# Channel shuffle on one core: eight buffers of 24 KB a partition become four of 48 KB, loaded whole and stored in halves, with the small tiles first

## The chip, the cores and the metric

One core of one Trainium2 chip runs the kernel. The time is the device time of one execution in microseconds (us), given as the median of the runs of one job; single runs of one kernel mostly agree within 0.3%. A profile records one such execution; its span is some 1.8 us shorter than the time. Ratios are the mean time of one kernel's fast runs over the mean of the other's fast runs in the same rounds on the same chip, with a 95% interval, so they are not quite the ratios of the medians that are quoted.

## The reference

The reference reorders channels: 65,536 rows (16 x 64 x 64) of 256 floats, in each of which 8 groups of 32 channels are interleaved.

```python
x = x.reshape(batch, h, w, groups, channels_per_group)   # 8 groups of 32
x = x.transpose(0, 1, 2, 4, 3)
x = x.reshape(batch, h, w, c)
```

No arithmetic is done. 67.11 MB are read and 67.11 MB written.

## The kernel before

Each tile takes 128 x q rows of x, q rows of 1 KB to a partition; in the text a "24 KB tile" is one with q = 24. SBUF and PSUM are two memories on the chip; a tile lies in SBUF, spread over 128 partitions. SP (the sync engine) issues the load. DVE (the vector engine) permutes 8 KB pieces from SBUF into PSUM, ACT (the scalar engine) copies them back in place, and ACT issues the store when all pieces of the tile are done. A DMA of a tile has 128 rows, one for each partition; a "row of 24 KB" below is such a row. In the packet records of the traces each row is one packet, and each DMA adds 16 packets of 4 bytes, here called completion writes, which tell its semaphore that the data have landed.

```python
_SIZES = [24] * 20 + [8, 24]
_BUFS = 8
_PIECE = 8
...
    for q in _SIZES:
        buf = pool.tile([P, biggest * c], F32, name="buf")
        nc.sync.dma_start(out=buf[:, : q * c], in_=rows(x_flat, first, q))
        for k in range(0, q, _PIECE):
            piece = buf[:, k * c : (k + _PIECE) * c]
            bounce = psum.tile([P, _PIECE * c], F32, name="bounce")
            nc.vector.tensor_copy(
                out=bounce.rearrange("p (i j g) -> p i j g", j=CPG, g=G),
                in_=piece.rearrange("p (i g j) -> p i j g", g=G, j=CPG),
            )
            nc.scalar.copy(out=piece, in_=bounce)
        nc.scalar.dma_start(out=rows(out_flat, first, q), in_=buf[:, : q * c])
```

A load into a buffer waits until the buffer's last store has landed. The 44 DMAs share eight completion semaphores (the landings in the trace), so a DMA may also have to wait for the one that had its semaphore last.

Of the kernel before, what the change touches and what calls it, by code (L numbers as in the profile page):

```python
# [1 line left out]

# [4 lines left out]


F32 = mybir.dt.float32
P = 128  # L10

_SIZES = [24] * 20 + [8, 24]
_BUFS = 8

_PIECE = 8


@with_exitstack
def kernel(
    ctx: ExitStack,  # L20
    tc: tile.TileContext,
    x: bass.AP,
    groups: bass.AP,
    out: bass.AP,
):
    nc = tc.nc
    b, h, w, c = x.shape
    G = int(groups)
    CPG = c // G
    assert G * CPG == c  # L30
    assert sum(_SIZES) * P == b * h * w
    biggest = max(_SIZES)

    x_flat = x.rearrange("b h w c -> (b h w c)")
    out_flat = out.rearrange("b h w c -> (b h w c)")

    pool = ctx.enter_context(tc.tile_pool(name="pool", bufs=_BUFS))
    psum = ctx.enter_context(
        tc.tile_pool(name="psum", bufs=2, space=bass.MemoryType.PSUM)
    )  # L40

    def rows(flat, first, q):

        return flat[first * c : (first + P * q) * c].rearrange("(p f) -> p f", p=P)

    ctx.enter_context(tc.manual_schedule(engines=None))
    first = 0
    for q in _SIZES:
        buf = pool.tile([P, biggest * c], F32, name="buf")
        nc.sync.dma_start(out=buf[:, : q * c], in_=rows(x_flat, first, q))  # L50
        for k in range(0, q, _PIECE):
            piece = buf[:, k * c : (k + _PIECE) * c]
            bounce = psum.tile([P, _PIECE * c], F32, name="bounce")
            nc.vector.tensor_copy(  # L54
                out=bounce.rearrange("p (i j g) -> p i j g", j=CPG, g=G),
                in_=piece.rearrange("p (i g j) -> p i j g", g=G, j=CPG),
            )
            nc.scalar.copy(out=piece, in_=bounce)  # L58
        nc.scalar.dma_start(out=rows(out_flat, first, q), in_=buf[:, : q * c])  # L59
        first += P * q  # L60


# [1 line left out]
_INS = ['x', 'groups']  # L64
_OUTS = [((16, 64, 64, 256), 'float32')]

_NUMBERS = {'groups': 8}


# [26 lines left out]
```

## Time and profile before

| | before |
|---|---|
| time, median of 3 | 317.66 us (317.65 to 317.87) |
| span of the profile | 315.9 us |
| DVE, ACT busy | 72%, 38% |
| both DMA queues, share of 16 engines | 99.3% |

The two queues are q1 (loads, issued by SP) and q10 (stores, issued by ACT). The list of waits of the compute engines (who waited for whom; us in total, times, longest; L58 is line 58 of the kernel) is worth a look, as it seems to say where time could be had:

```profile
ACT buf L58 <- DVE bounce L54: 115.3, 56, 5.6
ACT buf L58 <- DMA buf<-in_x_dram: 55.7, 4, 26.0
DVE bounce L54 <- ACT buf L58: 38.8, 4, 18.8
```

ACT once stood 26 us behind a load, and DVE then stood 18.8 us behind ACT.

### The profile page before, as it was taken

The page shows a single profiled execution, that of the slowest core. Times are in us where ns is not written, and L with a number is a line of the kernel's source. Part 1 is how long each engine was busy: PE and PEld are TensorE (multiplying, and loading weights), DVE is VectorE, ACT ScalarE, POOL GpSimd, SP SyncE. Part 2 cuts the span into 40 slices and gives each one's busy share as a digit, 9 for nine tenths or more (in the row PEclk, how much of TensorE's full clock was granted, in tenths as well). Part 3 has the DMA queues.
Part 4 walks back from the last instruction along what each step waited for, and adds up shares of the span by engine and source line. Part 5 has one row for each costly group of instructions (what it writes and reads, how often), then busy time and mean ns, then how long its engine had stood idle before and what let it go on. Part 6 is the DMA issues. An engine that isn't in the chain of part 4 may idle for free.

```text
span 315.9 us, 289 instructions
## 1 busy us (share of the span) xinstructions
DVE 227.9 (72%) x64; ACT 120.3 (38%) x65; POOL 0.2 (0%) x4
## 2 busy tenths in 40 slices
DVE  0699999959587685957008986999970299999900
ACT  0354455525252424330015416545500444555420
POOL 0000000000000000000000000000000000000000
DMA  8999999999999999999999999999999999999997
GB/s 296 439 442 380 436 429 433 433 439 433 423 442 433 426 442 426 426 442 426 433 436 427 433 436 436 433 426 437 433 423 448 423 429 444 429 423 433 439 432 302
DMA packets 6338, 134.24 MB, mean 425 GB/s; under 512 B 704, under 2 KB 704, under 8 KB 704
## 3 DMA queue, kind: packets, MB, share of 16 engines
q1 hardware_dynamic: 3168, 67.11, 49.9%
q10 hardware_dynamic: 3168, 67.11, 49.4%
q14 instruction: 2, 0.02, 0.0%
HBM read 67.11 MB, written 67.11 MB: 425 GB/s over the span
## 4 chain that ended last, share of the span: by engine, by line
DVE 54%; another core or an unknown queue 23%; issue 8%; ACT 5%; DMA 3%; DVEq 1%; ACTq 0%
DVE bounce L54 54%; ACT buf L58 5%; DMA buf<-in_x_dram 3%; DVEq L91 1%; ACTq L59 0%; DVEq L54 0%; ACTq L58 0%
## 5 line engine op out<-in xcount | busy, mean ns | idle before, releaser
L54 DVE COPY bounce<-buf 128x2048 f32<-128x2048 f32 x64 | 227.9, 3636 | 72.6 <-ACT buf L58 38.8
L58 ACT COPY buf<-bounce 128x2048 f32<-128x2048 f32 x64 | 119.0, 1866 | 171.1 <-DVE bounce L54 115.3
L58 ACT ACT_TABLE_LOAD x1 | 1.3, 1283 | 11.1 <-DMA buf<-in_x_dram 11.1
L77 POOL MEMSET const-bfloat16-1.0<- 128x1 bf16 x1 | 0.1, 102 | 0.0
L77 POOL MEMSET const-uint8-127<- 128x1 uint8 x1 | 0.1, 101 | 0.0
L77 POOL MEMSET const-float32-0.0<- 128x1 f32 x1 | 0.1, 99 | 0.2 <-issue 0.2
L77 POOL MEMSET const-float32-1.0<- 128x1 f32 x1 | 0.1, 98 | 0.0
## 6 DMA issues: line engine op xcount, KB each, us to landing
buf<-in_x_dram SPq DMA_DIRECT2D x21, 3072.0 KB, 58.4
out_dram<-buf ACTq DMA_DIRECT2D x21, 3072.0 KB, 24.2
buf<-in_x_dram SPq DMA_DIRECT2D x1, 1024.0 KB, 46.0
out_dram<-buf ACTq DMA_DIRECT2D x1, 1024.0 KB, 15.8
```

The source lines that it names most:

```text
L54: nc.vector.tensor_copy(out=bounce.rearrange("p (i j g) -> p i j g", j=CPG, g=G), in_=piece.rearrange("p (i g j) -> p i j g", g=G, j=CPG),)
L58: nc.scalar.copy(out=piece, in_=bounce)
L77: nc = _bacc.Bacc("TRN2", target_bir_lowering=False, num_devices=1)
L91: with _tile.TileContext(nc) as tc:
```

## The change

The intent is to issue fewer, longer loads, to let data flow out as soon as half a tile is ready, and to start computing earlier by taking the small tiles first. The bytes in SBUF stay 192 KB a partition.

```diff
-_SIZES = [24] * 20 + [8, 24]
-_BUFS = 8
+_SIZES = [8, 24] + [48] * 10
+_BUFS = 4
+
+_STORE = 24
 ...
-        for k in range(0, q, _PIECE):
-            ... permute a piece, copy it back
-        nc.scalar.dma_start(out=rows(out_flat, first, q), in_=buf[:, : q * c])
+        for a in range(0, q, _STORE):
+            b = min(a + _STORE, q)
+            for k in range(a, b, _PIECE):
+                ... permute a piece, copy it back
+            cols = slice(a * c, b * c)
+            nc.scalar.dma_start(
+                out=rows(out_flat, first, q)[:, cols], in_=buf[:, cols]
+            )
```

(The loop bodies are cut; they are the ones above. `b` of the shape is renamed to `n`.)

More of the change, by code (lines that the diff above doesn't have):

```diff
@@ L26 @@
     nc = tc.nc
-    b, h, w, c = x.shape
+    n, h, w, c = x.shape
     G = int(groups)
@@ L30 @@
     assert G * CPG == c
-    assert sum(_SIZES) * P == b * h * w
+    assert sum(_SIZES) * P == n * h * w
     biggest = max(_SIZES)
@@ L50 @@
         nc.sync.dma_start(out=buf[:, : q * c], in_=rows(x_flat, first, q))
-        for k in range(0, q, _PIECE):
-            piece = buf[:, k * c : (k + _PIECE) * c]
-            bounce = psum.tile([P, _PIECE * c], F32, name="bounce")
-            nc.vector.tensor_copy(
-                out=bounce.rearrange("p (i j g) -> p i j g", j=CPG, g=G),
-                in_=piece.rearrange("p (i g j) -> p i j g", g=G, j=CPG),
-            )
-            nc.scalar.copy(out=piece, in_=bounce)
-        nc.scalar.dma_start(out=rows(out_flat, first, q), in_=buf[:, : q * c])
+        for a in range(0, q, _STORE):
+            b = min(a + _STORE, q)
+            for k in range(a, b, _PIECE):
+                piece = buf[:, k * c : (k + _PIECE) * c]
+                bounce = psum.tile([P, _PIECE * c], F32, name="bounce")
+                nc.vector.tensor_copy(
+                    out=bounce.rearrange("p (i j g) -> p i j g", j=CPG, g=G),
+                    in_=piece.rearrange("p (i g j) -> p i j g", g=G, j=CPG),
+                )
+                nc.scalar.copy(out=piece, in_=bounce)
+            cols = slice(a * c, b * c)
+            nc.scalar.dma_start(
+                out=rows(out_flat, first, q)[:, cols], in_=buf[:, cols]
+            )
         first += P * q
```

## The prediction

> **What bounds the kernel now.** I read the page's strip of slices first, then the queues, then a table of stretches, the queues inside one short window, and last the waits of the load queue.
>
> ```profile
> span 315.9 us, 289 instructions
> DVE 227.9 (72%) x64; ACT 120.3 (38%) x65; POOL 0.2 (0%) x4
> ...
> DMA  8999999999999999999999999999999999999997
> ...
> q1 hardware_dynamic: 3168, 67.11, 49.9%
> q10 hardware_dynamic: 3168, 67.11, 49.4%
> ```
>
> DVE has 88 us to spare and ACT 195 us; the DMA row stands at 9 from the second slice to the last but one. Queue q1 (loads) and q10 (stores) together fill 49.9 + 49.4 = 99.3% of 16 engines over the span. The table of stretches (us, then busy time of DVE, ACT and POOL, clock, DMA share, GB/s) says where the rest is:
>
> ```profile
> 0.00:1.70 1.70, 0.00 (x0) 0.00 (x0) 0.20 (x4) 1.00 0.00 0
> 1.70:4.00 2.30, 0.00 (x0) 0.00 (x0) 0.00 (x0) 1.00 1.11 299
> 4.00:24.00 20.00, 12.95 (x4) 6.88 (x4) 0.00 (x0) 1.00 1.00 433
> 24.00:32.00 8.00, 8.00 (x3) 3.73 (x2) 0.00 (x0) 1.00 1.02 399
> 32.00:140.00 108.00, 85.89 (x25) 46.63 (x25) 0.00 (x0) 1.00 1.00 432
> 140.00:170.00 30.00, 10.48 (x3) 3.63 (x2) 0.00 (x0) 1.00 1.00 432
> ...
> 302.50:314.00 11.50, 0.00 (x0) 0.00 (x0) 0.00 (x0) 1.00 0.97 416
> 314.00:315.90 1.90, 0.00 (x0) 0.00 (x0) 0.00 (x0) 1.00 0.00 0
> ```
>
> The body runs at 432 GB/s whether loads run alone (4 to 24 us) or with stores. 134.2 MB at 432 GB/s is 310.7 us. Lost on top: 1.7 us before the first packet, 2.3 x (1 - 299/432) = 0.7 us of slow first packets, 8 x (1 - 399/432) = 0.6 us when stores set in, 0.4 us in the drain, 1.9 us after the last packet: 5.3 us, together 316.0 against a span of 315.9. Even between 140 and 170 us, where DVE works 10.48 of 30 us, DMA stays at 432. There ACT stands before a store: the built program has eight DMA completion semaphores, and a store that takes one over waits for the DMA that had it, here a load; the chain of waits has a hole of 25.46 us from 138.75. Loads fill that hole, so it costs nothing. The kernel is bound by DMA engines, and only those 5.3 us are not transfer.
>
> **How the two queues share an engine.** This decides the change, and the one 8 KB tile of the kernel before shows it. In a window in which that load runs against a store of 24 KB rows:
>
> ```profile
> q10 hardware_dynamic: 121, 2.58, 74.9%
> q1 hardware_dynamic: 113, 0.91, 26.8%
> ```
>
> Columns: packets, MB, share of 16 engines over 8 us (128 us of engine time). 2.58 MB are 105 rows of 24 KB, 0.91 MB are 111 rows of 8 KB: about one row of each in turn, while the bytes go 2.8 to 1. A row takes 0.749 x 128 / 105 = 0.913 us (24 KB) or 0.268 x 128 / 111 = 0.309 us (8 KB); the packet records read 912 and 309 ns. From the two: 603 ns for 16 KiB more is 37.7 ns a KiB, which leaves 309 - 8 x 37.7 = 7.5 ns a row. A 48 KB row should then take 48 x 37.7 + 7.5 ns = 1.82 us, if it goes as one packet.
>
> **What the Trainium skill says.** "DMA: Bandwidth & Descriptors", section "Queues, rings and completion order": each engine goes round-robin between queues at packet granularity. The trace agrees, and shows that a turn here is one row of the DMA (105 against 111), not the 9 to 17 descriptors that the page calls typical. Same page, "Where 436 GB/s comes from": a ceiling of 435.2 GB/s; the trace has 432 to 433, so there is under 1% to win in the body. Same page, "Why small descriptors are slow": a fixed cost for each packet; the trace has about 7.5 ns. "Perfetto Trace Analysis", section "DMA Optimizations": splitting DMAs may help "If DMA engines are generally idle"; here they are not, so splitting the store should not pay by itself.
>
> **The change part by part.**
> - Compute: the order of instructions shows the same 64 DVE copies (3.56 us from start to start) and 64 ACT copies (1.87 us). Nothing removed.
> - Bytes: the same. Loads: 21 of 24 KB rows and one of 8 KB become 10 of 48, one of 24, one of 8. Each engine has 8 of the 128 rows of a tile, so 160 rows of 24 KB become 80 of 48 KB: 80 x 7.5 ns = 0.6 us less. Ten fewer completion writes, 9 ns each in the packet records: 0.1 us less. Stores: 22 as before. Sum: **-0.7 us**.
> - Small tiles first: the first load (1 MB instead of 3) should land at about 11.0 - 8 rows x 0.603 = 6 us instead of 11, and the first store be issued at about 6 + 3.6 + 1.9 = 12 us instead of 23.7. It starts DVE 5 us earlier, beside a DMA queue that is full anyway: 0 us. The 1.7 and 1.9 us at the ends stay, the slow first packets too.
> - The end: a last tile of 48 KB instead of 24. It looks bad: DVE needs 6 x 3.56 = 21.3 us after its load. But a load is issued only when the tile four before it has been stored (in the program, load 12 waits for stores 13 and 14). Count from then, in time of one DMA engine: the six stores of tiles 9 to 11 are still to go, 6 x 7.3 = 43.8 us, and the last load, 8 x 1.82 = 14.6 us: 58.3 us of work that needs nothing from the last tile. Rows alternate, so the load is through after 8 x (1.82 + 0.91) = 21.8 us, and lands 3 us later at most (10.3 us for the first load of 7.3 us of rows). First half permuted at 24.8 + 10.7 + 1.9 = 37.4, second at 48.1. The engines come to them at 58.3 and 65.6. **Spare: some 20 and 17 us.** The end stays full.
> - The middle: the loads take two bytes for one of the stores, so a tile is loaded beside one of its two stores in 21.8 us, then 7.3 us of store alone: 29.1 us a tile, against 21.3 us of DVE. Loads get ahead until buffers stop them, as today; a queue always has work.
>
> Sum: 317.66 - 0.7 = **317.0 us**.
>
> **Rivals.**
> 1. *Loads and stores share bytes equally* (48 KB rows cut in pieces of 24 KB, or turns by bytes). Then loads lose their lead: the second store comes at about 26 us (second load landed at 13.5, three DVE copies, one ACT copy); until then loads, nearly alone, have moved about 70 KB a partition of 512 (21 us at 7.3 us for 24 KB). The other 442 at 14.6 us for 24 KB take 269 us, so the last load lands at some 291 to 295 us, as it never waits for a buffer. Then 21.3 + 1.9 us of permuting and 7.3 + 1.5 us for the last store: 323 to 327, most of it with idle engines. Time about **326**. Against it: the 8 KB rows above. For it: no row over 24 KB is in this trace.
> 2. *A new semaphore wait.* With 34 DMAs instead of 44 over eight semaphores the pairings change; a store held behind a load could leave both queues empty, since four buffers give loads fewer places. In the new program two stores take over a load's semaphore (store 14 after load 9, store 16 after load 10), both of loads issued four stores or more earlier. I expect waits of DVE and ACT, hidden as today; if one were bare, 5 to 10 us, 322 to 327.
> 3. *A faster start.* If an early store or shorter first load saved the lost start, at most the 1.3 us of slow packets: 315.7. Against it: the first packets wait whatever their length.
> 4. *DVE becomes the bound*: 228 us of 316; would need 80 us more. No.
>
> Load waits on stores exist already and are the throttle that keeps the order:
>
> ```profile
> SPq L50 <- DMA out_dram<-buf: 209.9, 14, 22.0
> ```
>
> 209.9 us of waiting in the load queue, with full engines: it costs nothing now, and should not after.
>
> **Range and chances.** The floor is 310 us of bytes plus about 5, so 2% less (311.3) is closed: 0.01. Rivals 1 and 2 together some 7%, and either makes it over 2% slower (324.0). The rest is within 2%. For the range: rival 3 and small row savings below (316.0), a us or two of gaps at buffer changes above (318.8).
>
> **What would show it.** Right: 1728 packets on q1 instead of 3168 (12 loads of 128 rows, and 16 completion writes each), two thirds of bytes to loads where both run, DMA at 432 to the last slices, the last load landing at about 265 us (73 us of engine work are left when it is issued, 58.3 and 14.6 for the last tile's stores, so that is at 314 - 73 = 241, and 24.8 more), the last store issued some 17 us before the engines come to it. Wrong: equal MB on q1 and q10 in every window, last load at 290 or later, zeros in the DMA row in the last three slices; or a hole in mid-run with ACT waiting before a store.

## The result, and the profile after

The changed kernel takes **317.78 us** (median of 4, 317.37 to 318.22), the kernel before 317.65 us in the same job. The ratio is 1.0003 (0.9986 to 1.0021): the same.

The changed kernel's page and its table of stretches (columns as in the prediction):

```profile
span 316.4 us, 251 instructions
DVE 228.0 (72%) x64; ACT 120.6 (38%) x65; POOL 0.2 (0%) x4
...
q1 hardware_dynamic: 1728, 67.11, 49.7%
q10 hardware_dynamic: 3168, 67.11, 49.3%
```

```profile
1.70:4.00 2.30, 0.00 (x0) 0.00 (x0) 0.00 (x0) 1.00 0.99 292
...
32.00:140.00 108.00, 99.83 (x29) 52.22 (x28) 0.00 (x0) 1.00 0.99 426
140.00:170.00 30.00, 22.21 (x7) 11.19 (x6) 0.00 (x0) 1.00 1.01 437
...
302.50:314.00 11.50, 0.00 (x0) 0.00 (x0) 0.00 (x0) 1.00 0.97 417
```

The number of load packets went from 3168 to 1728, so a row of 48 KB is one packet. The queues still fill 99.0% of the engines, start and drain have the rates of before (292 and 417 GB/s against 299 and 416), and the middle scatters from stretch to stretch (426, 437), but its mean from 4 to 302.5 us is 431 GB/s in both profiles. Within the bound, a lot did change. Over a stretch in which both queues always had work (52 to 92 us), the queues shared the engines like this (packets, MB, share):

```profile
q1 hardware_dynamic: 256, 11.80, 68.1%
q10 hardware_dynamic: 256, 5.51, 32.0%
```

Packets are equal in number and the loads have two thirds of the time. That holds only while a load is under way. Later a load is issued only when a buffer comes free, and over two whole tile periods (152.68 to 210.92 us, 29.1 us a tile as predicted) both queues move the same bytes:

```profile
q10 hardware_dynamic: 577, 12.61, 50.3%
q1 hardware_dynamic: 288, 12.58, 49.9%
```

So what the longer rows shorten is the flight of each load, after which its queue stands empty for some 7 us. The waits changed with it:

```profile
ACT buf L62 <- DVE bounce L58: 166.0, 64, 10.4
DVE bounce L58 <- DMA buf<-in_x_dram: 62.2, 12, 8.7
```

After its start ACT waits for DVE alone; the holds behind a load's semaphore are gone. DVE waits for each of the 12 loads, and for nothing else. The last load and the last tile, from the chain of waits and the timeline (start us, length us, what; ACTq is the queue from which ACT issues DMAs):

```profile
242.99 25.85 DMA buf<-in_x_dram
```

```profile
281.57 0.34 ACTq L64 DMA_DIRECT2D out_dram<-buf  x1
292.22 0.34 ACTq L64 DMA_DIRECT2D out_dram<-buf  x1
```

The load was issued at 242.99 us and landed at 268.84; the last two stores were issued at 281.57 and 292.22 us. By the packet records, the engines came to the rows of the last store at 306.4 us. It had been issued 14 us before it was needed.

### The profile page after: what moved, and what is told of

It reads as the page before. It is cut to its first block, busy times and chain, and to the rows that moved or that the text cites. A ratio compares the mean times of both kernels' runs of the same rounds, so it can differ in the third digit from the quotient of the medians.

```text
span 316.4 us, 251 instructions
## 1 busy us (share of the span) xinstructions
DVE 228.0 (72%) x64; ACT 120.6 (38%) x65; POOL 0.2 (0%) x4
## 3 DMA queue, kind: packets, MB, share of 16 engines
q1 hardware_dynamic: 1728, 67.11, 49.7%
q10 hardware_dynamic: 3168, 67.11, 49.3%
## 4 chain that ended last, share of the span: by engine, by line
another core or an unknown queue 46%; DMA 31%; DVE 12%; ACT 1%; DVEq 1%; SPq 1%; issue 0%
DMA buf<-in_x_dram 17%; DMA out_dram<-buf 13%; DVE bounce L58 12%; ACT buf L62 1%; DVEq L98 1%; SPq L52 1%; DVEq L58 0%
```

## The experiments

All kernels gave the correct output. The kernel before ran beside each group: 317.76, 317.63 and 317.55 us.

| run | what | time, us | ratio to before (95%) | last load landed | last store issued |
|---|---|---|---|---|---|
| changed kernel | | 317.78 | 1.0003 (0.9986 to 1.0021) | 268.9 | 292.2 |
| load_cut24 | load rows cut into two packets | 318.79 | 1.0034 (1.0019 to 1.0049) | 284.6 | 307.9 |
| load_two | two loads of 24 KB | 317.71 | 1.0002 (0.9987 to 1.0017) | 289.9 | 302.5 |
| tiny_load | 12 extra loads of 64 KB | 320.89 | 1.0104 (1.0083 to 1.0125) | 279.5 | 302.8 |
| tail_half | last tile: 3 more DVE copies | 318.11 | 1.0012 (0.9997 to 1.0027) | 269.1 | 303.3 |
| tail_twice | last tile: 6 more | 324.88 | 1.0216 (1.0198 to 1.0235) | 269.0 | 314.1 |
| tail_thrice | last tile: 12 more | 346.84, one run | | 268.6 | 335.5 |
| bufs3 | three buffers | 317.41 | 0.9988 (0.9973 to 1.0003) | 282.9 | 306.2 |
| bufs2 | two buffers | 371.32, one run | | 336.7 | 360.0 |
| before_small_first | before, small tile first | 317.59 | 0.9999 (0.9984 to 1.0014) | | 299.7 |
| store48 | one store a tile | 323.34 | 1.0185 (1.0168 to 1.0202) | 281.3 | 304.6 |
| halves_last | one store a tile, halves in the last two | 316.52 | 0.9966 (0.9952 to 0.9980) | 281.5 | 304.8 |
| after_again | the changed kernel, 5 rounds | 317.69 | 1.0009 (0.9997 to 1.0022) | 268.5 | 291.8 |

(The last two columns are us from the span's start in the profiled run; a load's landing is read from the start of the DVE copy that waited for it; in before_small_first none waited for the last.)

The theory had four parts: the DMA engines are the bound; they take one packet of each queue in turn, so rows of 48 KB against 24 KB give loads two thirds; loads therefore end early, and the permuting of a last tile of 48 KB has room before the engines come to its stores; the early start is worth nothing. The main rival was that packet size does not decide the share, and that the end is full for another reason.

### Is it the packet that takes the turn? load_cut24, tiny_load, load_two

**load_cut24** changes the row size and, but for the padding that this takes, nothing else: the buffer gets 64 bytes of padding after each half, so that each row of the load is two packets.

```diff
-        buf = pool.tile([P, biggest * c], F32, name="buf")
-        nc.sync.dma_start(out=buf[:, : q * c], in_=rows(x_flat, first, q))
+        buf = pool.tile([P, 2, _STORE * c + 16], F32, name="buf")
+        n_cut = max(1, q // _STORE)
+        part = q * c // n_cut
+        nc.sync.dma_start(
+            out=buf[:, :n_cut, :part],
+            in_=rows(x_flat, first, q).rearrange("p (s f) -> p s f", s=n_cut),
+        )
```

(The new indices of the pieces and stores, which follow from this, are cut.)

> The changed kernel, but each load row of 48 KB is cut into two packets of 24 KB (the buffer is padded by 64 bytes between its halves); same number of loads, same buffers, same waits. Theory (engines take one row of each queue in turn, so the 48 KB rows give loads two thirds of the bytes): now loads and stores share equally, 10.. 3008 packets on the load queue, last load lands at 288 to 295 us instead of 268.8, last store is issued at about 314 instead of 292, engines idle some 9 us before the end, time 324 to 328 us. Rival (turns go by whole DMA or by bytes, packet size does not matter): last load still near 269, time 317 to 319.

The first DVE copy of the last tile, which waited for its load:

```profile
284.60 21.35 DVE L63 COPY bounce<-buf 128x2048 f32<-128x2048 f32 x6 [6.80 <-DMA buf<-in_x_dram]
```

The last load was issued at 229.7 us, 13 us earlier than in the changed kernel, and yet landed at 284.6 us, 16 us later than there and not "near 269", so the rival falls. But it is 3 us earlier than the theory allowed, and the time is 318.79 us, 1 us over the kernel before and not 6 to 10. The queues over two whole tile periods (86.07 to 142.42 us):

```profile
q1 hardware_dynamic: 543, 12.56, 51.7%
q10 hardware_dynamic: 544, 11.80, 48.6%
```

Packets are equal, but bytes are not: 12.56 MB are 32 rows of 24 KB for each of the 16 engines, 11.80 MB are 30. The missing rows are completion writes. In these two periods the stores are four DMAs and the loads two, each ends in one 4-byte packet on each engine, and that packet takes a turn too: 32 + 2 turns for the loads, 30 + 4 for the stores. The theory had left this out. One row a tile, 0.91 us, over ten tiles is 9 us, which moves the 288 to 295 us told to 279 to 286; the load came at 284.6. After it 23.3 us of permuting follow, to the last store at 307.88 us, while the engines ran out of older stores from 306.7 to 308.6 us (packet records). That was nearly in time, and the loss is small.

**load_two** gives both queues the same packets and the same number of completion writes: each tile is loaded by two loads of 24 KB.

```diff
-        nc.sync.dma_start(out=buf[:, : q * c], in_=rows(x_flat, first, q))
+        for a in range(0, q, _STORE):
+            cols = slice(a * c, min(a + _STORE, q) * c)
+            nc.sync.dma_start(out=buf[:, cols], in_=rows(x_flat, first, q)[:, cols])
```

> The changed kernel with each 48 KB load issued as two loads of 24 KB rows, so that DVE may start on the first half when that has landed, and both queues have the same packets and the same number of completion writes. Theory (with a completion write taking a turn of its queue, the load queue got 15 of 31 rows too few turns lost in the cut load, and keeps an even share here): last 24 KB load lands at 288 to 293 us, later than in the cut load (284.6), but only half a tile has to be permuted after it; last store issued at 302 to 306, engines full to the end, time 317.3 to 318.5 us. Rival (one load of 48 KB is what holds the time): 319 or more.

(The clause on the cut load is garbled; it seems to mean the row a tile that the stores lost there.) Over two tile periods (60 to 118.2 us):

```profile
q10 hardware_dynamic: 576, 12.58, 50.2%
q1 hardware_dynamic: 576, 12.58, 50.2%
```

With as many DMAs on both sides, equal packets are equal bytes. The last load landed at 289.9 us, 5 us later than in load_cut24, in the direction and range told, with 22 DMAs on each side instead of 12 against 22. The landing has a second difference behind it (DVE starts on half tiles), so alone it would not show the turn of the completion write; the packet counts of the two runs do. Only three pieces are left to permute after it, and the time is the one of before.

**tiny_load** goes the other way: it adds turns without adding bytes.

```diff
         nc.sync.dma_start(out=buf[:, : q * c], in_=rows(x_flat, first, q))
+        extra = small.tile([P, 128], F32, name="extra")
+        nc.sync.dma_start(out=extra, in_=rows(x_flat, first, q)[:, :128])
```

(The pool `small`, with a buffer for each, is cut.)

> The changed kernel with one tiny extra load (128 rows of 512 B, 64 KB) behind each of its 12 loads. Theory (a turn of an engine is one packet of any size, the completion write counts as one too): each tiny load costs the load queue 9 turns of almost no bytes, so its 48 KB tile now needs 18 turns instead of 9 and loads lose their double share: last load lands at 283 to 292 us instead of 268.8, last store issued at 300 to 307 instead of 292, time 319 to 322 us (12 x 8 rows of some 27 ns are 2.6 us). Rival (shares go by bytes or by DMA, not by packets): last load lands at 270 to 273, time under 319.

While such a load was at its turn (248 to 254 us):

```profile
q10 hardware_dynamic: 118, 2.51, 97.1%
q1 hardware_dynamic: 116, 0.05, 3.0%
```

118 packets against 116 (rows and completion writes), and 50 times the bytes: a tiny packet of 27 ns was given the same turn as a row of 912 ns. The last load landed at 279.5 us, 10.6 us later than in the changed kernel for 0.8 MB more; that is more than the packets' own 2.7 us, but short of the 283 us told, and why it fell short was not looked into. The time, 320.89 us, is in the range told; most of the 3.1 us over the changed kernel is those 2.7 us, which the tiny packets take on each engine (12 loads x 8 rows x 27 ns, 2.6 us, and their completion writes).

### How much room has the end? tail_half, tail_twice, tail_thrice, bufs3, bufs2

In three kernels DVE copies of the last tile are repeated, with the same values written to the same place:

```diff
+                for _ in range(_AGAIN if first + P * q == n * h * w else 1):
                   nc.vector.tensor_copy(
```

(The rest of the call is cut. `_AGAIN` is 2 in tail_twice and 3 in tail_thrice; tail_half repeats only the first half's three pieces.)

> The changed kernel with the three DVE copies of the first half of the last tile done twice (same values): 3 x 3.56 = 10.7 us more DVE work in the tail. Theory (the last store is issued 292.2 us and the engines come to its rows at 306.4, so 12 to 14 us are to spare): no change, 317.3 to 318.3 us, last store issued at 302.9. Rival (the tail is on the path, and only looks hidden): up to 10.7 us more, 328.

> The same with all six DVE copies of the last tile done twice: 21.3 us more. Theory: last store issued at 313.5, 7 us after the engines would have come to it, and 1 to 4 us from issue to the first row: 325 to 329 us, that is the spare of 12 to 14 us is eaten and the rest shows. Rival (work there is free, or the spare is larger than told): under 322.

> The changed kernel with the six DVE copies of the last tile done three times, 42.7 us more. Theory (the spare is used up at some 14 us, and beyond it each us of DVE in the tail is a us of time: twice gave 7.1 us more for 21.3): 7.1 + 21.3 = 28 us more than the changed kernel, 345 to 347 us. Rival (something else grew with it): outside 343 to 349.

10.7 us more of DVE work cost 0.3 us over the changed kernel, within the noise of both. 21.3 us more cost 7.1 us, and 42.7 us more cost 29.1 us. So about 14 us are free and the rest shows in full: 21.3 - 14.2 = 7.1. In tail_twice the last store and two stretches show where it comes to light:

```profile
314.11 0.34 ACTq L67 DMA_DIRECT2D out_dram<-buf  x1
```

```profile
292.22:306.00 13.78, 13.71 (x5) 3.14 (x3) 0.00 (x0) 1.00 1.01 433
306.00:316.00 10.00, 6.14 (x2) 2.75 (x2) 0.00 (x0) 1.00 0.22 91
```

DVE works through 14 us in which the engines are full (433 GB/s); only after 306 us do they stand (91 GB/s), until the store that was issued at 314.11. tail_twice, 324.88 us, came just below the range told: the first row followed 0.84 us after the issue (packet records), not 1 to 4. tail_thrice, 346.84 us, is in its range.

The number of buffers tests the count behind this room: at the issue of the last load, the stores of one tile fewer are left for each buffer fewer.

```diff
-_BUFS = 4
+_BUFS = 3        # bufs3;  2 in bufs2
```

> The changed kernel with three buffers of 48 KB instead of four. Theory (by the same count: when the last load is issued four old stores are left, 29.2 us, and the load, 14.6 us: 43.7 us of engine work against 37.4 us until the first half of the last tile is permuted, 51 against 48): still full, with 3 to 6 us to spare, 317 to 320 us, last load issued at about 256. Rival (four buffers are what keeps the queues full): over 324.

> The changed kernel with two buffers of 48 KB. Theory (by the same count two old stores, 14.6 us, and the load, 14.6 us, are left when a load is issued: 29.2 us of engine work against 37.4 us until the first half of that tile is permuted): each tile leaves the engines idle for some us, 350 to 370 us, DVE waits for loads in every tile. Rival: under 330.

Three buffers are as good as four: 317.41 us. But the last store was issued at 306.15 us, its first rows moved at 307.0, and the engines had run out of older rows from 305.9 us on (packet records): nothing of the 14 us is left, where 3 to 6 us were told. With two buffers the time is 371.32 us, 1 us above the range told, and every tile shows the hole (60 us of mid-run, DVE waits):

```profile
200.00:260.00 60.00, 42.72 (x12) 22.38 (x12) 0.00 (x0) 1.00 0.91 370
```

```profile
DVE bounce L58 <- DMA buf<-in_x_dram: 130.2, 12, 15.5
```

The holes are not all of it. By the packet records, idle engines make some 37 of the 54 us over the changed kernel; the other 17 us are packets that took longer, above all rows of 48 KB, with a mean of 2.04 us instead of 1.83. Why those are slower with two buffers was not looked into, and the theory had no such term.

### Is the early start worth anything? before_small_first

```diff
-_SIZES = [24] * 20 + [8, 24]
+_SIZES = [8, 24] + [24] * 20
```

> The kernel before with only the order of its tiles changed: the small tile first, then 21 of 24 KB. Theory (an earlier first landing starts DVE beside a DMA queue that is full anyway): first copy at 5.5 us instead of 11.05, time within 0.3 us of before, 317.4 to 318.0. Rival (the start is on the path): 4 to 5 us less.

The first DVE copy starts at 5.57 us instead of 11.05, and the time is 317.59 against 317.63 us. As the DMA queues are full anyway, the earlier start of DVE is worth nothing here.

### Are the half stores worth anything? store48, halves_last, after_again

```diff
-_STORE = 24
+_STORE = 48
```

> The changed kernel with one store of 48 KB a tile instead of two of 24 KB. Theory: rows of 48 KB on both queues share evenly, the last load lands at 279 to 283 us, and the one last store starts only when all six pieces are done: 23.2 us after the landing, then 14.6 us of rows and 1.5 us: 321 to 325 us in all. Rival (halves of the store change nothing, as splitting does not pay where engines are full): 317 to 318.

One store a tile costs 5.7 us over the kernel before. The last load landed at 281.3 us (rows of 48 KB on both sides, even shares), and then (two stretches up to the issue of the last store):

```profile
281.35:299.00 17.65, 17.65 (x5) 7.46 (x4) 0.00 (x0) 1.00 0.93 401
299.00:304.64 5.64, 3.71 (x2) 3.73 (x2) 0.00 (x0) 1.00 0.00 0
```

For 5.64 us the engines have nothing at all, since the first half of the last tile, long done, has to wait for the second. halves_last halves only the stores of the last two tiles:

```diff
-        for a in range(0, q, _STORE):
-            b = min(a + _STORE, q)
+        half = _STORE if first + 2 * P * q >= n * h * w else q
+        for a in range(0, q, half):
+            b = min(a + half, q)
```

(here with `_STORE = 24`.)

> The kernel with one store of 48 KB a tile (323.3 us), but with the stores of its last two tiles halved again. Theory (the half stores matter for nothing but the last tile, which is permuted after the last load; in mid-run the engines are full anyway): back to 317 to 318.5 us, last store issued at 303 to 307 and engines full to the end. Rival (half stores matter in every tile, as buffers come free and rows share otherwise): 320 or more.

It takes 316.52 us, 6.8 us less than store48 and half a us below the range told: the half stores gain at the end and nowhere else; in the other tiles they seem to cost about 1 us. It is also better than both kernels, if only by 0.34% (0.20 to 0.48%) of the kernel before. Its profiled run took 318.41 us, while its five other runs lie between 316.39 and 316.66; so its profile is not one of its typical runs, and the gain is read from the times alone. The ratio is that of the five; with the sixth the mean would be 0.9977 of the kernel before.

> The changed kernel once more, unchanged, in five rounds, to see whether the 0.7 us of fewer row and completion costs is there. Theory of the prediction: 0.7 us faster than before, ratio 0.9978. Theory now: some 48 KB rows took longer than the usual 1.815 us in the profiled run, which gives it back: ratio 0.999 to 1.002.

The changed kernel once more: 1.0009 (0.9997 to 1.0022). The predicted 0.9978 is outside, the later 0.999 to 1.002 holds.

## Why the prediction was right or wrong

The prediction was right: 317.0 us told, 317.78 measured, in the range of 316.0 to 318.8 and within the 2% to which it gave 92%. Its terms of 0 us held; its one term that was not zero failed, and was too small to leave the range. By its steps:

- **The DMA engines are the bound** (right). They were full in both kernels, and DVE work added at the end was free exactly as long as they were full (tail_half, tail_twice).
- **Rows of 48 KB take the turns of rows of 24 KB** (right). 256 packets against 256 at 11.80 and 5.51 MB; cutting the rows moved the last landing by 16 us.
- **The count at the end** (right in kind, 3 us off in size). Told: last load issued at 241 us, landed 24.8 us later, last store ready 48.1 us after the issue, room 20 and 17 us. Measured: 243.0, 25.9, 49.2, and room of 17.6 and 14.2 us. 1.1 us of it is the load's flight. The other 2.2 us are in the start of the count: it assumed six whole stores left at the issue, but the packet records have the first rows of the next store at 241.0 us, 2 us before. Over a tile the count held (29.1 us told and measured).
- **The small tiles first are worth 0 us** (right). First copy 5.5 us earlier, first store issued at 11.0 us instead of 23.7, no time gained, and none either when done alone.
- **80 rows fewer and 10 completion writes fewer save 0.7 us** (this term failed). Nine runs of the changed kernel in two jobs show nothing of it: medians 317.78 and 317.69. It is not that the rows were mis-sized: most 48 KB rows take 1815 ns in the packet records, as estimated (1.82 us), and the sum of all packet times is 0.3 us an engine lower than before in the first profile and 0.9 us in the second. But the last data packet ends at 315.2 and 314.7 us in the two, against 314.6 us before. Counting the packets open at once shows where the saving went. Before, neighbouring records overlapped by 1.1 us an engine in all, after by 0.8, so 0.3 us of what the rows seemed to cost had been hidden in overlap. And the engines stood idle for 1.3 and 1.4 us instead of 0.7, all of the difference before 32 and after 300 us; between these it is 0.1 us in all three. What makes the ends longer is open. So is why halves_last gains 1.2 us over the changed kernel, when its further 64 rows and 8 completion writes would give 0.6: against the kernel before it gains 1.0 us, where the same costs add up to 1.2.
- **Splitting the store should not pay by itself** (wrong as a statement, with no term in the sum). It rested on the engines' not being idle. That is true of the run, but with whole stores not of its last 20 us: one store a tile costs 5.6 us over the changed kernel (store48).
- **Rival 1, even shares, "about 326 us"** (its mechanism right, its size wrong). Made on purpose, it gave 318.79 us. The step that failed is the landing at 291 to 295 us: it left out that a completion write takes a turn, which takes one row a tile from the stores when they are two DMAs to one load. With shares that are even in fact, in load_two, the last load landed at 289.9 us.
- **Rival 2, a new semaphore wait**, did not come: ACT waited for DVE alone. **Rival 3, a faster start**, did not come: 292 GB/s in the first packets against 299.

## What to carry to other kernels

In this kernel, with the DMA engines full, a fourth buffer, the order of the tiles and an early start were worth nothing (two buffers, which let the engines run empty, cost 54 us); what is left to ask is what stands between the last load's landing and the last store's issue, and whether older stores cover it. Count that in engine time, from the issue of the last load. The sizes of the rows on two queues, and the number of DMAs, set here how the queues shared the engines. Longer rows on the load queue shortened the flight of a load (25.9 us, against 54.9 us with cut rows), and the room so made covered three buffers instead of four, but no fewer.

## What the Trainium skill lacked or had wrong

- "DMA: Bandwidth & Descriptors", section "Queues, rings and completion order": it gives the round-robin at packet granularity, which the traces bear out, and some 9 to 17 descriptors as typical for a packet, which they cannot check, as they record packets alone. What it does not say is what a packet is for plain loads and stores like these: one row, whatever its size. 105 rows of 24 KB went against 111 of 8 KB, 256 packets of either queue with 11.80 and 5.51 MB, 118 packets against 116 where the rows had 24 KB and 512 B.
- The same section does not say that a completion write takes a turn of its queue. In load_cut24, 543 against 544 packets went with 12.56 and 11.80 MB, since the stores had twice as many DMAs; in load_two, with as many on both sides, 576 packets each went with 12.58 MB each.
- No page draws the consequence that row lengths set the shares of two queues: 68.1% and 32.0% with rows of 48 and 24 KB.
- "Perfetto Trace Analysis", section "DMA Optimizations": it says of splitting DMAs that the task as a whole may end sooner if the engines are generally idle. With whole stores (store48) they were 97% busy, and splitting the last two tiles' stores was still worth 6.8 us (323.34 and 316.52 us). The condition should be about the stage.
